# An encoder's ConvFFN on one core: partial sums seeded in PSUM, the down product in units between the up products

## The chip, the core and the metric

The kernel runs on one core of one Trainium2 chip. The metric is the device time of one execution in microseconds. TensorE's clock is granted at one of two levels, 1.2 or 2.4 GHz; the profile gives it as a share of the higher one.

## What is computed

Two layers of an encoder over 768 tokens of width 1024 (two requests of 512 and 256 tokens, six tiles of 128 tokens). Each layer has a mixer (latent attention beside a Fourier branch) and then the ConvFFN that the change touches:

```python
def conv_ffn(h, w_up, w_conv, b_conv, w_down):
    up = centred_dwconv(h @ w_up, w_conv, b_conv)
    a, b = jnp.split(up, 2, axis=-1)
    return (jax.nn.gelu(a, approximate=True) * b) @ w_down

h = rms_norm(x, g_ffn_pre[l]) * (1 + sc2) + sh2     # D_MODEL 1024, D_FF 2816
y = conv_ffn(h, w_up[l], w_conv[l], b_conv[l], w_down[l])
x = x + gt2 * rms_norm(y, g_ffn_post[l])
```

The scales, shifts and gates come from `silu(c) @ w_ada + b_ada`, six segments of 1024 columns per layer. All is float32; every product is made of three matmuls of split halves (high × high, high × low, low × high).

## The kernel before, in words

**Up products.** `ffn` works through 22 pairs `j` of 128 columns of `w_up`, one column block of the left half and one of the right. A pair is a two-by-two block product in seven products instead of eight: sums and differences of the four weight quarters (`up_weights`) times seven sums and differences of the input's quarters (`form_step`, kept in `S["FH"]`). A product (`prod` in `up_pair`) is 12 matmuls of up to 384 columns (L1311 to L1313) into one bank of PSUM. Products 0 and 2 share bank "a", 3 and 5 share "c", 1 is in "b", and 4 and 6 are in "d"; product 2 adds onto what 0 left in "a", product 5 onto what 3 left in "c", and product 6 onto "d". Between the two, the intermediate value is read out: `p1_` (ScalarE, L1334) copies the first sum to SBUF, `p6` (L1337), `p7` (L1343), `p5` (L1346), `p4` (L1349) and `p3` (L1354) are VectorE adds from PSUM and SBUF. Then come the convolution along the tokens (`conv`, L1224 to L1229) and `finish` (gelu, product, split), which leaves `G[j]`.

**Weights.** A pair's two raw blocks of `w_up` come by two transfers of 512 KB from the SyncE queue (L147). `l1x`, `s12`, `s3`, `s4` make four forms; three of them fill two blocks each (high part by ScalarE, L1258, low part by VectorE, L1259), the fourth fills one (L1281, L1282); the sums are on VectorE (L1267, L1268, L1273, L1278). Raw blocks, forms, down weights and several temporaries all come out of one pool of 20 blocks (`blk`, 128 x 1024 float32).

**Down product.** Every two pairs make a chunk (the last has four). `down_step` runs a chunk for one token tile into two fresh banks (L1389 to L1391), ScalarE copies the banks to a block (L1401) and GpSimd's queue adds the block onto `y_d` in DRAM (L1403 for the first chunk, L1405 after). A chunk's six steps stand behind the next pair's seven products. The last chunk reads `y_d` back (L501).

**Start and order.** The input's third column group (token tiles 4 and 5) is made late, by `h_last` (`form_step`: transposes L441, copies L444, sums and splits L453 to L463). So pairs 0 and 1 are split into a part of 256 and one of 128 columns, and `h_last` stands between pair 1's second and third product of 256 columns. Between the pairs stand "fillers", pieces of `ada_steps`, which form the scales and shifts on VectorE (L317, L319) from `w_ada` blocks.

`run` writes out the steps in this order, with the loads and splits of later weights in between: loads up to `RAWS` entries ahead, splits by a planned start (`LA_SPLIT`) and by how many blocks of the pool are free. Behind the first steps the framework orders the instructions of each engine by priority and readiness; on the chip each engine takes them in the order so fixed.

## Time and profile before

| | |
|---|---|
| three runs | 2407.21, 2408.55, 2416.14 us; median 2408.55 |
| profiled execution: its own time, its span | 2411.59 us, 2409.8 us |
| TensorE busy (matmul, weight load) | 96%, 86% of the span |
| VectorE, ScalarE, GpSimd busy | 67%, 45%, 10% |
| mean granted clock of TensorE | 0.971 |

Busy time is the share of the span in which the engine has an instruction under way. The matmuls of TensorE overlap in the rows, so what one costs is the distance from its start to the next one's. "Idle before" is the time in which the engine stood still ahead of an instruction, with the instruction whose end released it. All times are in us from the start of the span.

### The profile page before, as it was taken

The numbers are of one execution on the slowest core, as the hardware profiler recorded it, in microseconds if no ns is written. First come the engines' busy times: TensorE is split into PE (matmuls) and PEld (weight loads), VectorE is DVE, ScalarE is ACT, GpSimd is POOL, SyncE is SP. The second block draws the span as 40 slices with busy tenths as digits, with TensorE's granted clock in tenths as the row PEclk, the third lists the DMA queues.
The fourth block names the chain that finished last, engine by engine and source line by source line (L and its number), as shares of the span: only waits on it lengthen the run. The fifth ranks groups of instructions, "written<-read, shape, count | busy, mean of one in ns | idle before, by whom it ended". The sixth has DMA issues, their size and how long they took to land. (4 is left out here: it accounts for less than half of the span.)

```text
span 2409.8 us, 33324 instructions
## 1 busy us (share of the span) xinstructions
PE 2313.5 (96%) x12848; PEld 2072.9 (86%) x12848; DVE 1624.9 (67%) x2692; ACT 1076.8 (45%) x1844; POOL 249.1 (10%) x409
## 2 busy tenths in 40 slices
PE   8999999999999889989999999999999998999998
PEld 5888889988899788888878888899888998888897
DVE  5665557763767778777686755477637877766677
ACT  4423345541644444445454233355416445545452
POOL 1002000000111110111130020000001011011001
PEclk9999999999979999999999999999999799999999
DMA  9554431242236664656555544312423365556654
GB/s 260 151 170 134 133 104 32 71 156 94 88 97 180 158 166 114 149 135 146 142 184 151 171 134 133 104 32 68 158 95 97 93 181 147 116 113 145 151 123 175
DMA packets 262556, 316.24 MB, mean 131 GB/s; under 512 B 21436, under 2 KB 194150, under 8 KB 262397
## 3 DMA queue, kind: packets, MB, share of 16 engines
q1 hardware_dynamic: 240365, 235.85, 32.4%
q0 software_dynamic: 22032, 78.26, 14.8%
q8 instruction: 101, 1.65, 0.3%
q14 instruction: 58, 0.48, 0.1%
HBM read 225.89 MB, written 81.87 MB: 128 GB/s over the span
## 5 line engine op out<-in xcount | busy, mean ns | idle before, releaser
L1311 PE MATMUL ps<-d,w 128*128 128x384 f32 (+2 forms) x1344 | 463.0, 345 | 64.5 <-DVE r L1343 55.4
L1312 PE MATMUL ps<-d,w 128*128 128x384 f32 (+2 forms) x1344 | 458.7, 342 | 2.4 <-DVE d L454 2.4
L1313 PE MATMUL ps<-d,w 128*128 128x384 f32 (+2 forms) x1344 | 456.1, 341 | 0.0
L187 PE MATMUL ps<-d,w 128*128 128x512 f32 (+1 forms) x1152 | 393.4, 342 | 0.0
L188 PE MATMUL ps<-d,w 128*128 128x512 f32 (+1 forms) x1152 | 362.4, 337 | 0.0
L1311 PEld LDWEIGHTS ps<-d,w 128*128 128x128 f32 x1344 | 272.8, 203 | 77.7 <-DVE r L1343 60.8
L190 PE MATMUL ps<-d,w 128*128 128x512 f32 (+1 forms) x1152 | 296.4, 338 | 0.0
L159 DVE TENSOR_TENSOR w<-w,w 128x1024 fp32r<-128x1024 f32 (+3 forms) x164 | 192.3, 1178 | 141.6 <-ACT w L158 71.3
L1312 PEld LDWEIGHTS ps<-d,w 128*128 128x128 f32 x1344 | 273.2, 203 | 3.8 <-DVE d L454 2.8
L1313 PEld LDWEIGHTS ps<-d,w 128*128 128x128 f32 x1344 | 272.6, 203 | 0.0
L187 PEld LDWEIGHTS ps<-d,w 128*128 128x128 f32 x1152 | 216.2, 188 | 52.6 <-issue 3.4
L158 ACT ACTIVATE w<-w 128x1024 fp32r<-128x1024 f32 (+2 forms) x168 | 170.9, 1024 | 177.5 <-DVE w L159 47.2
L188 PEld LDWEIGHTS ps<-d,w 128*128 128x128 f32 x1152 | 216.6, 188 | 25.2
L1389 PE MATMUL ps<-w,d 128*128 128x512 f32 x528 | 206.1, 390 | 0.1
L1390 PE MATMUL ps<-w,d 128*128 128x512 f32 x528 | 206.0, 390 | 0.0
L1391 PE MATMUL ps<-w,d 128*128 128x512 f32 x528 | 205.7, 390 | 0.0
L319 DVE SCALAR_TENSOR_TENSOR w<-w,c,w 128x512 f32<-128x512 f32 x280 | 195.4, 745 | 11.7 <-DMA w<-in_w_ada_dram 11.7
L1259 DVE TENSOR_TENSOR w<-w,w 128x1024 fp32r<-128x1024 f32 x132 | 159.8, 1220 | 57.9 <-ACT w L1258 56.6
L1258 ACT ACTIVATE w<-w 128x1024 fp32r<-128x1024 f32 x132 | 137.2, 1054 | 126.2 <-DVE w L1268 70.7
L190 PEld LDWEIGHTS ps<-d,w 128*128 128x128 f32 x1152 | 178.3, 190 | 0.4
L1224 ACT ACTIVATE r<-r,v 128x768 f32<-128x768 f32 x88 | 90.6, 1030 | 175.5 <-DVE r L1349 127.3
L1401 ACT ACTIVATE w<-ps 128x512 f32<-128x512 f32 x216 | 126.6, 595 | 86.9 <-PE ps L1391 82.6
(253 smaller groups left out, 4118.7 us busy)
## 6 DMA issues: line engine op xcount, KB each, us to landing
y_d<-w POOLq DMA_DIRECT2D x108, 512.0 KB, 6.4
w<-in_w_up_dram SPq DMA_DIRECT2D x88, 512.0 KB, 5.5
w<-in_w_ada_dram SPq DMA_DIRECT2D x80, 512.0 KB, 4.3
w<-in_w_in_dram SPq DMA_DIRECT2D x48, 512.0 KB, 4.5
w<-in_w_down_dram SPq DMA_DIRECT2D x44, 512.0 KB, 5.7
xs<-w SPq DMA_DIRECT2D x18, 512.0 KB, 2.7
w<-xs SPq DMA_DIRECT2D x18, 512.0 KB, 4.6
w<-in_w_ada_dram SPq DMA_DIRECT2D x32, 256.0 KB, 5.6
```

Of the source, the lines that this page charges most:

```text
L158: nc.scalar.activation(out=o_(w.hi), in_=i_(w.raw), func=AF.Copy)
L159: (w.eng or nc.vector).tensor_sub(out=o_(w.lo), in0=i_(w.raw), in1=f(o_(w.hi)))
L187: nc.tensor.matmul(o, lh, rh[:, c0:c0 + s], start=(first and k == 0), stop=False)
L188: nc.tensor.matmul(o, lh, rl[:, c0:c0 + s], start=False, stop=False)
L190: nc.tensor.matmul(o, ll, rh[:, c0:c0 + s], start=False, stop=(last and k == n - 1))
L319: nc.vector.scalar_tensor_tensor(out=o, in0=x, scalar=c, in1=o, op0=ALU.mult, op1=ALU.add)
L1311: nc.tensor.matmul(ps, wh[:, k], x, start=(start and k == 0), stop=False, skip_group_check=True)
L1312: nc.tensor.matmul(ps, wh[:, k], y, start=False, stop=False, skip_group_check=True)
L1313: nc.tensor.matmul(ps, wl[:, k], x, start=False, stop=(k == 3), skip_group_check=True)
L1389: nc.tensor.matmul(ps, gh[:, cc], dw[j].hi[:, o], start=(j == all_js[0]), stop=False)
L1390: nc.tensor.matmul(ps, gh[:, cc], dw[j].lo[:, o], start=False, stop=False)
L1391: nc.tensor.matmul(ps, gl[:, cc], dw[j].hi[:, o], start=False, stop=(j == all_js[-1]))
```

## The change

- `up_weights` makes seven forms instead of four, each in one block (high part in the left half, low part in the right), each made and freed by itself.
- The order of the seven products of a pair is a, c, b, a, d, b, d. Their banks are held for the whole FFN. `p1_` copies bank a into bank b by ScalarE, and the next product adds onto it there; `p6` copies b into d in the same way; `p5` copies c to SBUF; `p7` and `p3` are VectorE adds with it, `p2` and `p4` plain ScalarE copies. `base` runs one matmul into b and one into d ahead of their first use in an FFN.
- Pair 1 is not split by columns any more, and `h_last` stands between the two parts of pair 0.
- The down product of each chunk but the last is cut into 12 units (a token tile and a half of the columns), which stand between the up products of the next two pairs, in three banks that are held. A unit of a later chunk begins with a ScalarE copy of its partial sum from SBUF into the bank and ends with a copy back; `Y`, six blocks, stays in SBUF, and `y_d` is gone. Its down weights come by halves, a block for two pairs.
- `ada_steps` takes `w_ada` in eight parts of 128 rows and 1024 columns instead of 256 rows and 512 columns.
- `form_step` makes its seven splits in the new order of the products.
- The pool has 21 blocks instead of 20, the pool of rows 6 instead of 7. `run` counts outstanding loads by blocks (`RAWS` 4, a pair counts 2, its later forms 0), and splits ahead of time only while four blocks (`SLACK`) are free.

```diff
-R_BUFS = 7
+R_BUFS = 6
-W_BUFS = 20
+W_BUFS = 21
+SLACK = 4
-RAWS = 3
+RAWS = 4
...
-    y_d = [[dp.tile([128, D], F32, name=f"y_d_{l}_{t}") for t in range(NT)] for l in range(L)]
...
-        ws = [[w_rows(a["w_ada"][l], 2 * i, 2, seg * D + half * 512, 512) for i in range(4)] for half in range(2)]
+        ws = [w_rows(a["w_ada"][l], k, 1, seg * D, D) for k in range(8)]
...
             def load():
                 for i, w in enumerate(A):
                     w_dma(w)
                     box[i] = w.raw
                     w.raw = None
-            us[0].load = load
+            us[0].load, us[0].raws = load, 2
             for u in us[1:]:
-                u.load = lambda: None
-
-            def two(u, z):
-                u.hi, u.lo = blk(F32R), blk(F32R)
-                nc.scalar.activation(out=u.hi, in_=z, func=AF.Copy)
-                nc.vector.tensor_sub(out=u.lo, in0=z, in1=f(u.hi))
...
+                u.load, u.raws = lambda: None, 0
+
+            def put(i, z):
+                w = us[i].home = blk(F32R)
+                us[i].hi, us[i].lo = w[:, 0:512], w[:, 512:1024]
+                nc.scalar.activation(out=us[i].hi, in_=z, func=AF.Copy)
+                nc.vector.tensor_sub(out=us[i].lo, in0=z, in1=f(us[i].hi))
+
+            def l11():
+                put(0, box[0][:, 0:512])
+
+            def s1():
+                z = box[2] = blk(F32)
+                nc.vector.tensor_add(out=z[:, 0:512], in0=box[1][:, 0:512], in1=box[1][:, 512:1024])
+                put(1, z[:, 0:512])
...
+                def base(name):
+                    if name not in PB:
+                        w = us[0].hi
+                        PB[name] = bank()
+                        nc.tensor.matmul(PB[name][:, 0:384], w[:, 0:128], w[:, 0:384], start=True, stop=True)
+                    return PB[name][:, 0:n]
+
                 def p1_(ps):
+                    nc.scalar.activation(out=base("b"), in_=ps, func=AF.Copy)
+
+                def p5(ps):
                     B["t"] = row(F32)
-                    B["u2"], B["u3"] = B["t"][:, 0:n], B["t"][:, 384:384 + n]
-                    nc.scalar.activation(out=B["u2"], in_=ps, func=AF.Copy)
+                    B["p5"] = B["t"][:, 0:n]
+                    nc.scalar.activation(out=B["p5"], in_=ps, func=AF.Copy)
 
                 def p6(ps):
-                    nc.vector.tensor_add(out=B["u2"], in0=ps, in1=B["u2"])
+                    nc.scalar.activation(out=base("d"), in_=ps, func=AF.Copy)
...
                 def p7(ps):
-                    nc.vector.tensor_add(out=B["u3"], in0=ps, in1=B["u2"])
...
+                    nc.vector.tensor_add(out=half(1, 1), in0=q3(ps), in1=q3(B["p5"]))
 
                 def p3(ps):
-                    nc.vector.tensor_add(out=half(0, 1), in0=q3(ps), in1=q3(B["u2"]))
+                    nc.vector.tensor_add(out=half(0, 1), in0=q3(ps), in1=q3(B["p5"]))
                     B.clear()
                     if end:
                         conv(j, 0, C.pop(0))
+
+                def p4(ps):
+                    nc.scalar.activation(out=half(1, 0), in_=q3(ps), func=AF.Copy)
+                    if end:
+                        conv(j, 1, C.pop(1))
                         finish(j)
...
-                return [prod("a", 0, 0, 0, True, p1_), prod("b", 1, 512, 1, True, p6), prod("a", 0, 512, 2, False, p2, (0,)),
-                        prod("c", 2, 0, 3, True, p7), prod("d", 1, 0, 4, True, p5, (1,)),
-                        prod("c", 2, 512, 5, False, p4, (2,)), prod("d", 3, 0, 6, False, p3, (3,))]
+                return [prod("a", 0, 0, True, p1_), prod("c", 1, 4, True, p5), prod("b", 2, 1, False, p6),
+                        prod("a", 3, 2, False, p2), prod("d", 4, 3, False, p7), prod("b", 5, 6, False, p3),
+                        prod("d", 6, 5, False, p4)]
...
+        def down_unit(c, i):
...
+            js = list(range(starts[c], starts[c + 1]))
+            t, half = i % 6, i // 6
+            dc = dwc[c][half]
+
+            def emit():
+                if c == 0:
+                    if i < 3:
+                        YB.append(bank())
+                    if t not in Y:
+                        Y[t] = blk(F32)
+                ps = YB[i % 3]
+                y = Y[t][:, half * 512:half * 512 + 512]
+                if c:
+                    nc.scalar.activation(out=ps, in_=y, func=AF.Copy)
...
+                nc.scalar.activation(out=y, in_=ps, func=AF.Copy)
...
-        early = [up_pair(j, uw[j], ((0, 2), (2, 3))) for j in range(2)]
-        out += early[0][0] + early[1][0][0:2] + [h_last] + early[1][0][2:] + early[0][1] + early[1][1]
...
+        early = up_pair(0, uw[0], ((0, 2), (2, 3)))
+        out += early[0] + [h_last] + early[1] + up_pair(1, uw[1])[0]
+        units = []
+        for j in range(2, NF):
+            st = up_pair(j, uw[j])[0]
+            if j % 2 == 0 and first[j - 2] < lc:
+                units = [down_unit(first[j - 2], i) for i in range(12)]
+            slots = [0, 0, 0, 1, 2, 1, 1] if j % 2 == 0 else [1] * 7
+            for i in range(7):
+                out.append(st[i])
+                for _ in range(slots[i] if units else 0):
+                    out.append(units.pop(0))
+                if i in (2, 6):
+                    out += fillers.pop(0) if fillers else []
...
-                due = k <= i + 1 or start[k] - now <= LA_SPLIT
+                due = k <= i or (k <= i + 1 or start[k] - now <= LA_SPLIT) and free_blocks() >= SLACK
...
-            while nd < len(order) and nd - ns < (RAWS if not s.hold else s.hold):
+            while nd < len(order) and (sum(w.raws for _, w in order[ns:nd]) + order[nd][1].raws
+                                       <= (RAWS if not s.hold else s.hold)):
```

## Rows read from the trace of the kernel before

**Rows 1.** The profile's page, its first line.

```profile
span 2409.8 us, 33324 instructions
```

**Rows 2.** Stage table: stretch, length, busy time (instructions) per engine, granted clock, DMA.

```profile
622.00:700.00 78.00, 73.27 (x429) 70.66 (x428) 64.56 (x105) 44.90 (x76) 11.20 (x14) 0.78 0.25 75
700.00:1190.00 490.00, 446.68 (x2266) 412.00 (x2266) 369.70 (x553) 229.78 (x315) 59.17 (x77) 0.95 0.60 150
...
1250.00:1830.00 580.00, 580.00 (x3399) 508.03 (x3398) 350.26 (x630) 230.93 (x467) 44.59 (x93) 1.00 0.38 114
1830.00:1905.00 75.00, 68.12 (x402) 65.46 (x401) 58.43 (x95) 41.69 (x72) 10.52 (x12) 0.77 0.33 98
1905.00:2375.00 470.00, 451.14 (x2347) 418.87 (x2346) 339.07 (x505) 236.32 (x323) 47.05 (x58) 0.99 0.58 143
```

**Rows 3.** TensorE's waits, 700 to 1190, then 1905 to 2375: total, times, longest.

```profile
PE ps L1311 <- DVE r L1343: 37.9, 7, 7.0
PE ps L1311 <- ACT r L1334: 3.3, 3, 1.8
...
PE ps L1311 <- DVE r L1343: 17.5, 9, 4.8
```

**Rows 4.** Timeline of TensorE, 780 to 793: start, duration, instruction, idle before.

```profile
786.78 0.69 PE L1311 MATMUL ps<-d,w 128*128 128x384 f32 x1 [5.26 <-DVE r L1343]
787.27 0.52 PE L1312 MATMUL ps<-d,w 128*128 128x384 f32 x1
787.59 0.52 PE L1313 MATMUL ps<-d,w 128*128 128x384 f32 x1
...
791.08 0.33 PE L1313 MATMUL ps<-d,w 128*128 128x384 f32 x1
...
792.99 0.33 PE L1312 MATMUL ps<-d,w 128*128 128x384 f32 x1
```

**Rows 5.** Timeline of VectorE, 780 to 787.

```profile
782.43 0.69 DVE L1267 TENSOR_TENSOR w<-w 128x512 f32<-128x512 f32 x1 [5.00 <-DMA w<-in_w_up_dram]
...
786.18 0.55 DVE L1343 TENSOR_TENSOR r<-ps,r 128x384 f32<-128x384 f32 x1
```

**Rows 6.** Waits of SyncE's load queue, 700 to 1190, then 1905 to 2375.

```profile
SPq L147 <- DMA y_d<-w: 114.1, 15, 19.7
...
SPq L147 <- DMA y_d<-w: 213.8, 15, 26.5
```

**Rows 7.** ScalarE's groups by line, 1905 to 2375: busy, mean ns, idle before.

```profile
L1401 ACT ACTIVATE w<-ps 128x512 f32<-128x512 f32 x108 | 64.1, 595 | 54.2 <-PE ps L1391 51.9
L1258 ACT ACTIVATE w<-w 128x1024 fp32r<-128x1024 f32 x56 | 57.8, 1053 | 28.2 <-DMA w<-in_w_up_dram 14.5 <-DVE w L1268 11.3 <-issue 1.5
...
L1281 ACT ACTIVATE w<-w 128x512 fp32r<-128x512 f32 x19 | 11.9, 628 | 16.9 <-DMA y_d<-w 15.8 <-DVE w L1259 1.1
...
L1334 ACT ACTIVATE r<-ps 128x384 f32<-128x384 f32 x19 | 9.0, 475 | 2.5 <-PE ps L1313 2.5
```

**Rows 8.** Timeline of TensorE at the start of layer 0's FFN, 640 to 702.

```profile
643.78 0.28 PE L1313 MATMUL ps<-d,w 128*128 128x256 f32 x1
...
646.66 0.28 PE L1313 MATMUL ps<-d,w 128*128 128x256 f32 x1
649.87 0.66 PE L441 MATMUL ps<-ident,w 128*128 128x128 f32 x4 [2.93 <-DVE w L493]
...
659.55 0.22 PE L1311 MATMUL ps<-d,w 128*128 128x128 f32 x1
...
670.06 0.41 PE L1311 MATMUL ps<-d,w 128*128 128x128 f32 x1
670.27 0.41 PE L1312 MATMUL ps<-d,w 128*128 128x128 f32 x1
...
693.10 0.63 PE L1311 MATMUL ps<-d,w 128*128 128x384 f32 x1
```

More of the change, by code (lines that the diff above doesn't have):

```diff
@@ L337, in finish @@
                                     in_=bg[64 * half:64 * half + 64:32, 0:512])
-        return [part(h, i) for h in range(2) for i in range(4)], Step(finish, 0.9)
+        return [part(k) for k in range(8)], Step(finish, 0.9)
     def ada_groups(*segs):
@@ L1244, in up_weights @@
             box = {}
-            us = [Weight([], 0) for _ in range(4)]
+            us = [Weight([], 0) for _ in range(7)]
             def load():
@@ L1272, in s3, with s2, l12 @@
+            def s2():
+                z = box[2]
+                nc.vector.tensor_sub(out=z[:, 512:1024], in0=z[:, 0:512], in1=box[0][:, 0:512])
+                put(2, z[:, 512:1024])
+            def l12():
+                put(3, box[0][:, 512:1024])
             def s3():
-                nc.vector.tensor_sub(out=box[1][:, 0:512], in0=box[0][:, 0:512], in1=box[1][:, 0:512])
-                two(us[2], box.pop(1))
+                z = box[1][:, 0:512]
+                nc.vector.tensor_sub(out=z, in0=box[0][:, 0:512], in1=z)
+                put(4, z)
@@ L1301, in part, with prod @@
                 B = {}
-                def prod(name, u, o, i, start, after=None, free=()):
+                def prod(name, u, i, start, after):
                     def emit():
-                        if start:
-                            B[name] = bank()
-                        ps = B[name][:, 0:n]
-                        (wh, wl), (xh, xl) = form(u, o), S["FH"][i]
+                        if name not in PB:
+                            PB[name] = bank()
+                        ps = PB[name][:, 0:n]
+                        wh, wl = (z.rearrange("p (k c) -> p k c", k=4) for z in (us[u].hi, us[u].lo))
+                        xh, xl = S["FH"][i]
                         for k in range(4):
@@ L1394, in emit @@
                     dw[j].hi = dw[j].lo = None
-                if c == lc:
-                    return
-                for t in ts:
-                    ps = S.pop(("yp", t))
-                    y = blk(F32)
-                    for half in range(2):
-                        nc.scalar.activation(out=y[:, half * 512:half * 512 + 512], in_=ps[half], func=AF.Copy)
-                    if c == 0:
-                        nc.gpsimd.dma_start(out=y_d[l][t], in_=y)
-                    else:
-                        nc.gpsimd.dma_start(out=y_d[l][t], in_=y, accum_op=ALU.add)
@@ L1406, in down_step @@
[L1406 removed]
+            return Step(emit, 6 * len(js) * len(ts) * 512 * MM_US, [dw[j] for j in js])
+        YB = []
+        dwc = [[Weight([((j - starts[c]) * 512, 512, a["w_down"][l][j * 128:(j + 1) * 128, h * 512:h * 512 + 512], None)
+                        for j in range(starts[c], starts[c + 1])], 1024) for h in range(2)] for c in range(lc)]
+        def down_unit(c, i):
[12 more added lines that the diff above has]
+                    nc.scalar.activation(out=ps, in_=y, func=AF.Copy)
+                cc = slice(t * 128, t * 128 + 128)
+                for j in js:
+                    o = slice((j - js[0]) * 512, (j - js[0]) * 512 + 512)
+                    gh, gl = G[j]
+                    nc.tensor.matmul(ps, gh[:, cc], dc.hi[:, o], start=(c == 0 and j == js[0]), stop=False,
+                                     skip_group_check=True)
+                    nc.tensor.matmul(ps, gh[:, cc], dc.lo[:, o], start=False, stop=False, skip_group_check=True)
+                    nc.tensor.matmul(ps, gl[:, cc], dc.hi[:, o], start=False, stop=(j == js[-1]),
+                                     skip_group_check=True)
+                nc.scalar.activation(out=y, in_=ps, func=AF.Copy)
+                if t == 5:
+                    dc.hi = dc.lo = None
+                if i == 11:
+                    for j in js:
+                        G.pop(j)
+                    if c == lc - 1:
+                        YB.clear()
+            return Step(emit, 3 * len(js) * 512 * MM_US, [dc])
```

94 lines of the change are left out of this document (30 added, 64 removed).

## The prediction, made before the changed kernel was run

> **What bounds the kernel now.** I read the stage table first [rows 2], then who makes TensorE wait in the two stretches where it waits [rows 3], then one such wait instruction by instruction on TensorE [rows 4] and on VectorE [rows 5], then what holds up the loads [rows 6], ScalarE [rows 7], and last the start of the FFN [rows 8].
>
> The stage table says that TensorE sets the time. Between the two FFNs (1250 to 1830) it is busy in all 580 us, at the full granted clock; nothing that the change does there can help, and it can only hurt if it takes work's cover away. The holes are in the FFNs: 490.00 − 446.68 = 43.3 us of layer 0's steady part and 470.00 − 451.14 = 18.9 us of layer 1's, and the two starts (622 to 700, 1830 to 1905) run at a mean clock of 0.78 and 0.77 [rows 2].
>
> Nearly all of the 62 us has one cause. TensorE, at an up product's first matmul (L1311), waits for the VectorE add L1343: 7 waits and 37.9 us in layer 0, 9 waits and 17.5 us in layer 1 [rows 3]. The reader should see why that add is so urgent. Products 3 and 5 of a pair share bank "c", so product 5 may not write until `p7` (L1343) has read what product 3 left; only product 4 lies between. A product is 12 matmuls 0.1735 us apart (eleven steps from 791.08 to 792.99) [rows 4], so the cover is 2.08 us. At 782.43 VectorE had just stood still for 5.00 us, with L1267 at its head, a sum over the second `w_up` block, whose load had not landed; L1267, three more sums and a split ran, and only then L1343, at 786.18 [rows 5]. TensorE resumed at 786.78, after 5.26 us idle, and on the lower clock: the matmuls start 0.32 us apart (787.27, 787.59) and are back at 0.17 by 791.08 [rows 4]. Some 11 of them at 0.32 instead of 0.1735 cost another 1.6 us. Why the load is late: the load queue stood for 114.1 us of layer 0's stretch and 213.8 us of layer 1's waiting for a `y_d` transfer, which held the block that the load was to go into [rows 6].
>
> **The change, part by part.**
>
> *Down partial sums.* 108 accumulating `y_d` transfers go, and with them the waits of [rows 6] as they stand; six blocks of the pool now hold `Y` for the whole FFN, against one block more in the pool. So the loads lose a slow partner and also some room. The last chunk no longer reads `y_d` back.
>
> *Wait of product 5.* In the new order, (a, c, b, a, d, b, d), each second use of a bank again has one product between, so the cover is the same 2.08 us. But the reader in between is now ScalarE three times (`p1_` copies a into b before product b; the same copy frees a; `p6` copies b into d before product d) and VectorE once (`p7` before the last d). The three adds `p6`, `p4` and old `p7` leave VectorE, at 0.55 us each [rows 5]. No weight sum stands in front of the ScalarE copies; weight copies that wait for loads do.
>
> What can be won here is what [rows 3 and 4] show: layer 0, 37.9 + 7 × 1.6 = 49.1 us; layer 1, 17.5 us and two waits long enough to drop the clock (1.6 each), 20.7 us. Sum 70 us.
>
> *The start.* Pair 1 is no longer split into a 256- and a 128-column part. In the trace the 128-column products run from 659.55 to 693.10, 33.6 us for 168 matmuls; on the low clock they go 0.21 us apart (670.06, 670.27) [rows 8]. One pair's 84 of them on the low clock are 17.9 us. Against that, pair 1's 84 matmuls of 384 columns take 84 × 0.1735 = 14.6 us, plus 1.6 us until the clock is back. But cover goes: pair 1's first two products (24 matmuls from 643.78 to 646.66, 2.88 us) ran ahead of `h_last` and its other five behind it, while ScalarE and VectorE made the third column group. Now TensorE reaches the transposes 2.9 us sooner, and they start when their rows are ready, at 649.87 as now; the idle time of 2.93 us becomes 5.8 us. Then nothing runs until `split(0)` has ended, by my estimate at about 658, a little before the 659.55 of now, since pair 1's splits no longer mix in. So: 658 + 17.9 + 16.2 = 692.1, against 693.1; if the clock stays high in the narrow part (84 × 0.12 at most, 10.1 us), 683 and less. Layer 1 is the same picture. Bounds per layer: a loss of 5 us (one more wait of the kind in [rows 4]) and a gain of 11 us. I take +3 each, near the low-clock end, because that is what this trace's narrow matmuls did: 6 us.
>
> *ScalarE's load.* In layer 1's stretch it is busy 236.32 of 470 us [rows 2]. Per pair come three more product copies at 0.475 us (L1334), six preloads of a PSUM bank, and seven half-size weight copies at 0.628 (L1281) for three of 1.053 (L1258) and one of 0.628. The preload, a copy from SBUF into PSUM, is in no row; its cost lies between nothing and the 0.628 of L1281, and I take L1401's 0.595, which has the same 512 columns through PSUM the other way [rows 7]. Together 1.43 + 3.57 + 0.61 = 5.6 us per pair, 112 us in 20 pairs: ScalarE goes from 50% to about 77% of a stretch of 450 us. It stays below TensorE, but is no longer idle half of the time when a product ends.
>
> ScalarE's own waits for loads matter now as VectorE's did. In layer 1 they come to 14.5 us (L1258) and 15.8 us (L1281) [rows 7], 30.3 us, and I put layer 0 at the same, 60 us in both. A copy of 0.475 us behind such a wait has 2.08 − 0.475 = 1.6 us of cover. If loads stay as late as now and about half of the waiting is under that cover, 30 us are left; if they come early enough, nothing. Loads start further ahead (four blocks outstanding, counted as blocks) and have no `y_d` beside them, but the pool is tighter: half, 15 us.
>
> The Trainium skill (TensorE: Matmul & The Clock Gate, section "Architectural detail: the array is 16× 32×32, not 1× 128×128") says that ScalarE and VectorE take instructions strictly first in, first out; the trace agrees for VectorE, where an add with its data long there stood behind a sum without. By that rule a copy behind a waiting weight copy can't overtake it, and the 15 us would be nearer to the 30.
>
> *What stays on VectorE.* `p7` and `p3`, and `finish(j)`: the down units of a chunk now start after four products of the next pair (8.3 us after the pair that they need has ended), where before they started after all seven. VectorE is busy 369.70 of 490 us in layer 0 [rows 2], and in a stretch that is 40 us shorter with 1.65 us less per pair it is at about 75%. Bounds: none, or as much per wait as layer 1 shows now, 17.5 / 9 = 1.9 us, in each of 20 chunks, 39 us. I take half, 20 us.
>
> *The rest at nothing:* the two dummy matmuls per FFN of `base` (0.3 us each, among the idle time at the start); ada parts in half as many instructions over the same columns, VectorE work in stretches where TensorE is fully busy; `R_BUFS` 6, the `SLACK` rule and `RAWS` in the mixer and attention, hidden under TensorE's 580 busy us. Should that cover go, one wait as in [rows 4] costs 7 us.
>
> *Sum:* 70 + 6 − 15 − 20 = 41 us. The profiled execution took 2411.6 us for a span of 2409.8 [rows 1], so 2370.6 for its like; the median shown is 3 us lower: **2367 us**.
>
> **The rivals.**
>
> *ScalarE becomes the queue that TensorE waits for (slower).* Place: `p1_` and `p6`, each between two products with 2.08 us of cover. For it: 77% load, first in first out, and preload, evacuation, weight copies and the identity pass of the convolution (1 us pieces) all in that queue. Against it: TensorE's present waits for ScalarE are short, 3 of them and 3.3 us in layer 0 [rows 3]. If each of the two copies ends late by one weight copy and itself (1.053 + 0.475 = 1.53 us) in all 44 pairs, that is 134 us against the 76 of gain: 2408 + 58 = 2466 us. It decides from 76 / 44 = 1.7 us of new waiting per pair.
>
> *The load stays late.* In layer 0 the ada loads share the pool with `Y`; with six blocks gone for good the next `w_up` load again waits for a block and VectorE's sum again for the load. For it: the queue waits in [rows 6] are for blocks, not for bandwidth. Against it: a block held by a transfer is what goes away. Then layer 0's 49 us stay, and 21 + 6 − 20 is left: 2401 us.
>
> *The waits go altogether.* 70 + 6 and nothing new: 2332 us. For it: ScalarE has slack; against it: each pair has four turns of one bank between engines.
>
> **How the numbers follow.** The forecast 0.60, ScalarE 0.15, the load 0.13, all gone 0.12. The range goes from just under the full gain to just above no change, 2330 to 2412: it leaves out most of the ScalarE case and a twentieth below. The forecast's own range is 2340 to 2392, from the two halves that I took going to either bound. A measurement of this kernel can tell about 0.5% (12 us) from no change: faster 0.74 (the forecast, all gone, and a third of the load case), same 0.11, slower 0.15.
>
> **What would show it.** Right: no TensorE wait over 3 us in the two steady stretches, and no clock below 0.97 there; idle TensorE under 25 us in the two; the 128-column matmuls half as many, with a longer hole ahead of them; no `y_d` transfers; ScalarE at 70 to 80% in the steady part. Wrong: waits of an up product for a ScalarE copy of more than 1 us in most pairs (ScalarE rival), or L1267's successor standing for a `w_up` load with the load queue waiting for matmuls or splits to free a block (load rival). The prediction also fails if the mixer's stretch is longer than its 580 us, which would be the pool sizes and the new rule for splits.

## The result, and the profile after

The changed kernel takes 2314.0 us (median of 4 runs, 2312.1 to 2316.4) against 2410.0 us: ratio 0.9599, 95% interval 0.9578 to 0.962. That is 96 us faster, more than twice the 41 us forecast and below the low end of the range.

The profile's page begins with the span, 97.2 us shorter than in [rows 1]:

```profile
span 2312.6 us, 32983 instructions
```

The stage table of the changed kernel, cut at its own stages, answers to [rows 2]:

```profile
622.00:700.00 78.00, 71.26 (x386) 67.32 (x385) 60.73 (x98) 48.83 (x96) 10.16 (x14) 0.85 0.26 82
700.00:1130.00 430.00, 430.00 (x2263) 397.46 (x2262) 343.80 (x509) 314.16 (x525) 12.05 (x23) 1.00 0.34 100
1190.00:1770.00 580.00, 580.00 (x3399) 507.94 (x3399) 340.68 (x568) 232.93 (x474) 44.72 (x80) 1.00 0.39 118
1771.00:1840.00 69.00, 61.29 (x334) 59.60 (x333) 60.00 (x94) 41.91 (x81) 6.54 (x8) 0.80 0.25 81
1840.00:2280.00 440.00, 440.00 (x2313) 409.42 (x2312) 311.46 (x476) 316.87 (x531) 3.89 (x7) 1.00 0.27 81
```

Both steady stretches are full: 430 of 430 us and 440 of 440 us of TensorE at the full clock. ScalarE is busy 73% and 72% of them, VectorE 80% and 71%. What is left of TensorE's waits answers to [rows 3]; these are the four longest sums from 622 us to the end (three more, 4.0 us together, are ahead of transposes, L393), and all of them lie in the starts and the tails:

```profile
PE ps L439 <- DVE w L491: 5.0, 3, 4.3
PE ps L1315 <- ACT d L451: 3.4, 2, 3.2
PE ps L1315 <- ACT ps L1341: 3.3, 3, 1.6
PE ps L1315 <- DVE r L1355: 2.5, 1, 2.5
```

The start of layer 0's FFN on TensorE's timeline, for [rows 8]:

```profile
646.47 1.12 PE L439 MATMUL ps<-ident,w 128*128 128x128 f32 x4 [4.27 <-DVE w L491]
...
653.25 0.33 PE L1315 MATMUL ps<-d,w 128*128 128x128 f32 x1
...
670.29 0.41 PE L1317 MATMUL ps<-d,w 128*128 128x128 f32 x1
670.51 0.63 PE L1315 MATMUL ps<-d,w 128*128 128x384 f32 x1
...
673.17 0.49 PE L1317 MATMUL ps<-d,w 128*128 128x384 f32 x1
673.49 0.35 PE L1315 MATMUL ps<-d,w 128*128 128x384 f32 x1
...
694.84 0.39 PE L1430 MATMUL ps<-w,d 128*128 128x512 f32 x1
```

The 84 narrow matmuls that are left take 17.3 us (653.25 to 670.51), where the 168 took 33.6. The first down matmul stands behind four products (8.3 us) of pair 2, so that pair began at 686.5.

ScalarE's groups in 1840 to 2280, for [rows 7]; L1425 is the seed written into PSUM, L1341 the copy of one bank into another:

```profile
L1258 ACT ACTIVATE w<-w 128x512 fp32r<-128x512 f32 x131 | 81.1, 625 | 14.4 <-PE ps L1317 7.7 <-DVE w L1266 3.1 <-DVE w L160 1.5
L1435 ACT ACTIVATE w<-ps 128x512 f32<-128x512 f32 x107 | 63.1, 590 | 40.4 <-PE ps L1433 40.2
L1425 ACT ACTIVATE ps<-w 128x512 f32<-128x512 f32 x96 | 57.4, 598 | 1.9
...
L1341 ACT ACTIVATE ps<-ps 128x384 f32<-128x384 f32 x19 | 9.2, 483 | 1.3 <-PE ps L1317 1.3
```

No idle time of ScalarE in the two steady parts ends with a transfer any more.

**Where the 97 us came from.** From the first up matmul to the start of pair 2 (here the first down matmul less 8.3 us): 6.3 us in layer 0, 5.9 in layer 1. From there to the end of each FFN: 61.8 and 26.0 us. The mixer and attention between the FFNs became 3.1 us longer (598.3 to 601.4, from layer 1's first mixer matmul to its first up matmul). Before the first FFN 0.3 us. The sum is 97.2. For the largest part, one window from pair 2 to the end of each FFN, of the kernel before and then of the changed one:

```profile
693.10:1238.37 545.27, 500.23 (x2518) 458.94 (x2518) 410.08 (x619) 257.28 (x372) 78.78 (x100) 0.95 0.59 151
1900.24:2409.80 509.56, 482.89 (x2481) 445.17 (x2481) 370.29 (x564) 247.91 (x351) 53.52 (x71) 0.98 0.56 141
```

```profile
686.50:1170.00 483.50, 482.14 (x2518) 442.82 (x2517) 382.09 (x568) 340.59 (x581) 29.22 (x46) 1.00 0.34 104
1829.08:2312.60 483.52, 475.73 (x2482) 440.29 (x2480) 347.19 (x540) 331.62 (x565) 10.56 (x20) 1.00 0.26 82
```

TensorE's idle time fell from 45.0 to 1.4 us and from 26.7 to 7.8 us; the same number of matmuls took 18.1 us less in layer 0 and 7.2 us less in layer 1. The trace's record of the granted clock accounts for this: in these two windows of the kernel before, TensorE worked 37.5 and 12.6 us at 1.2 GHz, behind many of its waits and at the start of pair 2, half of which is lost against 2.4 GHz; in the changed kernel it did no work at that level there. So 62.6 us are waiting and 25.3 us are slow matmuls.

### The profile page after: what moved, and what is told of

The parts are those of the page before. It is cut to its first block, busy times and chain, and to the rows that moved or that the text cites. A ratio compares the mean times of both kernels' runs of the same rounds, so it can differ in the third digit from the quotient of the medians.

```text
span 2312.6 us, 32983 instructions
## 1 busy us (share of the span) xinstructions
PE 2273.0 (98%) x12684; PEld 2035.8 (88%) x12684; DVE 1557.9 (67%) x2516; ACT 1250.2 (54%) x2302; POOL 165.8 (7%) x301
## 5 line engine op out<-in xcount | busy, mean ns | idle before, releaser
L1315 PE MATMUL ps<-d,w 128*128 128x384 f32 (+2 forms) x1288 | 435.1, 338 | 9.3 <-ACT d L451 3.4
L1316 PE MATMUL ps<-d,w 128*128 128x384 f32 (+2 forms) x1288 | 434.5, 337 | 0.1
L1317 PE MATMUL ps<-d,w 128*128 128x384 f32 (+2 forms) x1288 | 433.3, 336 | 0.0
L1315 PEld LDWEIGHTS ps<-d,w 128*128 128x128 f32 x1288 | 251.1, 195 | 23.0 <-ACT d L451 4.2
L188 PEld LDWEIGHTS ps<-d,w 128*128 128x128 f32 x1152 | 216.2, 188 | 52.6 <-issue 3.4
L1316 PEld LDWEIGHTS ps<-d,w 128*128 128x128 f32 x1288 | 251.0, 195 | 9.6 <-DVE d L452 0.3
L159 ACT ACTIVATE w<-w 128x1024 fp32r<-128x1024 f32 (+2 forms) x168 | 171.5, 1024 | 159.9 <-DVE w L317 31.6
L1259 DVE TENSOR_TENSOR w<-w,w 128x512 fp32r<-128x512 f32 x308 | 206.4, 686 | 69.1 <-ACT w L1258 67.0
L1317 PEld LDWEIGHTS ps<-d,w 128*128 128x128 f32 x1288 | 251.0, 195 | 0.9 <-DVE w L1259 0.8
L189 PEld LDWEIGHTS ps<-d,w 128*128 128x128 f32 x1152 | 216.6, 188 | 25.7 <-DVE d L195 0.6
L1258 ACT ACTIVATE w<-w 128x512 fp32r<-128x512 f32 x308 | 189.1, 626 | 45.2 <-PE ps L1317 17.0
L317 DVE SCALAR_TENSOR_TENSOR w<-w,c,w 128x1024 f32<-128x1024 f32 x140 | 174.1, 1276 | 15.1 <-DMA w<-in_w_ada_dram 15.0
L191 PEld LDWEIGHTS ps<-d,w 128*128 128x128 f32 x1152 | 178.2, 190 | 0.2
L1435 ACT ACTIVATE w<-ps 128x512 f32<-128x512 f32 x216 | 127.5, 590 | 86.9 <-PE ps L1433 86.0
L1433 PE MATMUL ps<-w,d 128*128 128x512 f32 x432 | 171.3, 397 | 0.0
L1432 PE MATMUL ps<-w,d 128*128 128x512 f32 x432 | 170.5, 395 | 0.0
L1430 PE MATMUL ps<-w,d 128*128 128x512 f32 x432 | 167.6, 389 | 0.0
L1225 DVE SCALAR_TENSOR_TENSOR r<-r,v,r 128x511 f32<-128x511 f32 (+1 forms) x176 | 100.6, 613 | 34.1 <-ACT r L1222 33.9
```

The lines of the kernel that those rows point to most:

```text
L188: nc.tensor.matmul(o, lh, rh[:, c0:c0 + s], start=(first and k == 0), stop=False)
L189: nc.tensor.matmul(o, lh, rl[:, c0:c0 + s], start=False, stop=False)
L191: nc.tensor.matmul(o, ll, rh[:, c0:c0 + s], start=False, stop=(last and k == n - 1))
L1258: nc.scalar.activation(out=us[i].hi, in_=z, func=AF.Copy)
L1259: nc.vector.tensor_sub(out=us[i].lo, in0=z, in1=f(us[i].hi))
L1315: nc.tensor.matmul(ps, wh[:, k], x, start=(start and k == 0), stop=False, skip_group_check=True)
```

## The experiments

The theory after the result: the sum that no longer goes through DRAM frees blocks, so loads come in time and the two queues that feed TensorE no longer stand. Rivals: the finer weight blocks, the order and seeds of the products, the counting of loads, the rule of four free blocks (`SLACK`), the pools, the modulation's loads, the units spread between products.

### One part of the change undone

**Loads counted by entries.**

```diff
-RAWS = 4
+RAWS = 3
...
-            us[0].load, us[0].raws = load, 2
+            us[0].load = load
```

> The changed kernel, with one part undone: outstanding loads are counted by entries again, three at a time, a pair's later forms included. Load theory (the long waits went because the w_up blocks now land before their first reader): ScalarE and VectorE stand again for w_up loads, TensorE idles 20 us or more in the two steady parts, 2335 to 2400 us. Turn theory (they went because ScalarE instead of a VectorE add stands between two uses of a bank): a late load still has to block ScalarE's queue, but the copies are mostly ahead of it; 2314 to 2325 us. Cover theory (the down units between the products give the readers more time): like the turn theory, under 2325 us.

Measured 2311.0 us, ratio 0.9581 (0.9554 to 0.9609). The counting is worth nothing here.

**Units in one piece behind the pair.**

```diff
-            slots = [0, 0, 0, 1, 2, 1, 1] if j % 2 == 0 else [1] * 7
+            slots = [0] * 6 + [12 if j % 2 == 0 else 0]
```

> The changed kernel with all 12 down units of a chunk in one row behind the next pair, as before, instead of between the products. Cover theory: the seven products of a pair stand back to back again with 2.08 us between two uses of a bank, and preload and evacuation of the units follow each other on ScalarE in the row (1.2 us per unit of 1.36 us); waits of 1 to 3 us come back in most pairs, 2340 to 2400 us. Load theory and turn theory: within 10 us of the changed kernel, 2314 to 2325 us.

Measured 2317.5 us, ratio 0.9609 (0.9581 to 0.9636). The 3 us more lie within the two intervals; no long wait returned.

**Old order of the products, with VectorE's additions in fresh banks.**

```diff
-                return [prod("a", 0, 0, True, p1_), prod("c", 1, 4, True, p5), prod("b", 2, 1, False, p6),
...
+                return [prod("a", 0, 0, True, p1_), prod("b", 2, 1, True, p6, (1,)), prod("a", 3, 2, False, p2),
```

> The changed kernel with the old order of the seven products, the old VectorE adds and fresh banks a, b, c, d for each pair; forms in one block each, down units, loads counted by blocks and start stay. Turn theory: the wait for the add between products 3 and 5 comes back, VectorE has 1.65 us more per pair; 2340 to 2400 us. Load theory and cover theory: the adds find their turn in time, 2314 to 2330 us.

Measured 2314.4 us, ratio 0.9596 (0.9568 to 0.9623), with VectorE busy 86% of 700 to 1130 us and TensorE all of it. Not the cause by itself.

**Weight forms in pairs of blocks.**

```diff
-            us = [Weight([], 0) for _ in range(7)]
+            us = [Weight([], 0) for _ in range(4)]
...
-            for u, fn in zip(us, (l11, s1, s2, l12, s3, s4, l22)):
+            for u, fn in zip(us, (l1x, s12, s3, s4)):
```

> The changed kernel with one part undone: the weight forms of an up pair again in four steps, three of them with a block for the high and a block for the low halves of two forms, freed only when the later form is used. If the finer blocks are what keeps the loads and splits of the next pair on time, PE's waits in the steady parts come back and the run lands near 2380 us or above. If the sum that no longer goes through DRAM is enough by itself, PE stays busy through 700 to 1130 us and the time stays within 0.5% of 2314 us.

Measured 2320.6 us, ratio 0.961 (0.9595 to 0.9624): nothing that stands clear of the changed kernel's interval.

**The sum through the DRAM scratch again.**

```diff
-                    nc.scalar.activation(out=ps, in_=y, func=AF.Copy)
...
+                        nc.gpsimd.dma_start(out=y_d[l][t], in_=y, accum_op=ALU.add)
...
+                            Y[t] = load_x(y_d[l][t])
...
+                pend = [down_step(first[j], [t]) for t in range(NT)]
```

> The changed kernel with one part undone: the sums of the down products again go out by GpSimd's accumulating transfers to the DRAM scratch, a whole chunk behind the next pair, from blocks of the pool, and are read back for the last chunk; forms, seeds of the up products, start and counting of loads are those of the changed kernel. If those transfers are the cause (blocks held until they have landed, and the queues shared with the loads), the waits of PE in the steady parts come back and the run takes 2375 to 2400 us. If the block per form is the cause, it stays within 0.5% of 2314 us.

Measured 2319.6 us (2311.2 to 2324.1), ratio 0.9597 (0.9572 to 0.9623). The edit also puts the chunk back in one piece and its down weights back in rows. This fells my theory in its simple form. Its stage row, 700 to 1130, and then the time that its load queue stood for the sum's transfers, there and in 1900 to 2270:

```profile
700.00:1130.00 430.00, 425.59 (x2232) 393.13 (x2231) 335.90 (x499) 258.03 (x424) 54.83 (x73) 1.00 0.67 167
```

```profile
SPq L149 <- DMA y_d<-w: 117.8, 14, 29.4
SPq L149 <- DMA y_d<-w: 36.9, 10, 7.9
```

In layer 0 the load queue stands for the sum's transfers as long as in [rows 6]; in layer 1 it stands 36.9 us, where the kernel before has 184.1 in the same stretch. The 108 transfers land in 6.4 us (median) as they did, and a `w_up` load needs 5.9 us where it needed 5.5 in the kernel before (4.3 in the changed one). Yet TensorE is idle only 4.4 us in layer 0. That a queue working ahead stands for a block doesn't say that anyone needs the block soon.

**The start cut as before.**

```diff
-        early = up_pair(0, uw[0], ((0, 2), (2, 3)))
-        out += early[0] + [h_last] + early[1] + up_pair(1, uw[1])[0]
+        early = [up_pair(j, uw[j], ((0, 2), (2, 3))) for j in range(2)]
+        out += early[0][0] + early[1][0][0:2] + [h_last] + early[1][0][2:] + early[0][1] + early[1][1]
```

> The changed kernel with the start of each FFN undone: pair 1 is again cut into 256 and 128 columns around the last step of the forms. If the start is worth what the two traces say (6.3 and 5.9 us), it takes 2326 us, ratio to the kernel before about 0.965. If those 12 us come from the loads and not from the cut, it stays at 2314 us.

Measured 2331.6 us, ratio 0.9656 (0.9642 to 0.9671): 17.6 us above the changed kernel by the medians, which come from two rounds, some 14 us by the ratios, with the steady parts full. In the traces its two starts are 10.5 and 6.0 us longer than the changed kernel's. The start is a part of the gain of its own.

**No rule of four free blocks.**

```diff
-                due = k <= i or (k <= i + 1 or start[k] - now <= LA_SPLIT) and free_blocks() >= SLACK
+                due = k <= i + 1 or start[k] - now <= LA_SPLIT
```

> The changed kernel with one part undone: a split that is due within a step or 10 us is again put into the queues of ScalarE and VectorE whether or not four blocks are free. If the rule is what keeps those two queues from standing behind a block that is not free yet, PE's waits in the steady parts come back: 2360 to 2400 us. If it is not needed, since the blocks are free anyway, 2314 us within 0.5%.

Measured 2314.8 us, ratio 0.9601 (0.9586 to 0.9616). Not needed by itself.

### One part alone put into the kernel before

**Loads counted by blocks** (the reverse of the first edit).

> The kernel before, with one part done alone: outstanding loads counted by blocks, four at a time, a pair counts two and its later forms nothing. Load theory: most of the 7 waits of 5 to 7 us in layer 0 go; 2340 to 2370 us, against 2410. If it is the y_d transfers that hold the blocks, counting can't help, as the load queue waits for the block anyway: 2390 to 2415 us. Turn theory and cover theory: no gain, 2400 us or more.

Measured 2411.5 us, ratio 0.9989 (0.9977 to 1.0001): nothing in time. But what the engines stand for has changed. The largest waits for transfers of ScalarE and VectorE in 700 to 1130, in the kernel before and then in this run (L1259 and L1260 are its split):

```profile
ACT w L1258 <- DMA w<-in_w_up_dram: 24.4, 8, 7.6
DVE w L1267 <- DMA w<-in_w_up_dram: 17.1, 5, 5.5
```

```profile
ACT w L1259 <- DMA y_d<-w: 35.6, 8, 8.0
DVE w L1260 <- DMA y_d<-w: 18.5, 5, 5.5
```

The loads are there in time, and now the splits stand for a block that the sum's transfers hold.

**The sum kept on the chip.** Forms, products, loads, start and pools stay.

```diff
-                        nc.gpsimd.dma_start(out=y_d[l][t], in_=y, accum_op=ALU.add)
...
+                if c:
+                    nc.scalar.activation(out=ps, in_=y, func=AF.Copy)
...
+                pend = [down_unit(c, i) for i in range(12)]
```

> The kernel before with one part of the change alone: the sum of the down products stays in six blocks on the chip and is put into three held PSUM banks by ScalarE, the twelve units of a chunk in one piece behind the next pair; forms, products, loads, start and pools are those of the kernel before. If the transfers of the sum are the whole cause, the waits are gone and only the start (12 us) is missing: 2322 to 2340 us. If a block per form is needed as well, since six blocks fewer are left for weights, it stays near or above the kernel before, 2390 to 2430 us.

Measured 2362.9 us, ratio 0.9786 (0.9772 to 0.9801). Its steady parts are nearly full:

```profile
700.00:1130.00 430.00, 423.88 (x2201) 384.87 (x2200) 353.52 (x534) 269.30 (x400) 11.52 (x22) 1.00 0.32 96
1900.00:2270.00 370.00, 369.43 (x1924) 338.51 (x1923) 274.29 (x403) 247.11 (x366) 1.15 (x2) 1.00 0.25 75
```

That is between the two outcomes. Alone it takes away most of the waiting, though in the changed kernel it could be missed. Both can be true only if other parts of the change do the same work. The run also pays at its end: 23.0 us pass after its last matmul, where the kernel before and the changed kernel have 7.7 and 7.8. The two blocks of the last gate are loaded from 2336.51, when VectorE's add (L1457) releases them; the changed kernel issues these loads at 2272.43 and 2284.41, 40 and 28 us before its end.

```profile
2336.51 1.18 POOL L371 DMA_DIRECT2D w<-mod_d  x2 [0.86 <-DVE w L1457]
```

Without these 15 us the part alone would, as an estimate, be worth some 67 us instead of 52.

**The rule of four free blocks.**

> The kernel before with one part of the change alone: splits wait in the plan until four blocks are free, unless the step itself needs them. If the rule is the cause by itself, only the start (12 to 17 us) is missing: 2326 to 2345 us. If the blocks are short because the sum's transfers hold them, the rule has nothing to give and may put the splits later still: 2400 to 2440 us.

Measured 2414.7 us, ratio 1.0011 (0.9997 to 1.0025): nothing.

**A block per weight form** (with the counting by blocks).

> The kernel before with a block per weight form (and the loads counted by blocks, which alone was worth nothing: ratio 0.9989); order and additions of the products, the sum's transfers, start and pools as before. If the blocks that come free earlier are enough by themselves, 2330 to 2360 us. If the sum's transfers are what holds the loads, 2395 to 2412 us.

Measured 2377.0 us, ratio 0.9858 (0.9842 to 0.9874), between the two outcomes. In layer 1 the waits are all but gone (367.70 of 370 us busy from 1900), in layer 0 they are not (402.05 of 430 from 700). One of those left, on ScalarE's timeline and then on TensorE's:

```profile
941.55 1.15 ACT L1261 ACTIVATE w<-w 128x512 fp32r<-128x512 f32 x2 [3.90 <-DMA y_d<-w]
942.61 0.47 ACT L1339 ACTIVATE r<-ps 128x384 f32<-128x384 f32 x1
```

```profile
943.13 0.69 PE L1318 MATMUL ps<-d,w 128*128 128x384 f32 x1 [6.16 <-ACT r L1339]
```

Two weight splits (L1261) stand at the head of ScalarE for 3.90 us until a transfer of the sum gives back the block that the first of them writes into. Behind them stands the copy `p1_` (L1339), and TensorE waits 6.16 us for that copy. It is [rows 4 and 5] again, with the block in place of the load and ScalarE in place of VectorE.

**The sizes of the pools.**

```diff
-R_BUFS = 7
+R_BUFS = 6
...
-W_BUFS = 20
+W_BUFS = 21
```

> The kernel before with the sizes of the two pools alone: 21 blocks and 6 rows in place of 20 and 7. If the kernel before stood so close to the edge of its blocks that one more is enough, 2360 to 2385 us, and the waits of its queue of loads on the transfers of the sum shrink. If the pools are not it, 2405 to 2417 us, and the modulation's loads, or several of the small parts together, are left.

Measured 2434.2 us, ratio 1.0102 (1.0085 to 1.0118): 24 us slower, neither of the two outcomes expected. All of it is in layer 1, whose FFN is 28.8 us longer (layer 0's is 4.0 shorter):

```profile
700.00:1130.00 430.00, 394.70 (x2015) 363.25 (x2014) 329.49 (x498) 198.00 (x276) 50.35 (x68) 0.96 0.61 150
1900.00:2270.00 370.00, 339.33 (x1735) 315.66 (x1734) 255.34 (x376) 175.26 (x244) 35.61 (x44) 0.96 0.56 130
```

In that stretch the split of the down weights (L158) stands for the sum's transfers, which it never did there in the kernel before (11.5 us, all for its own load). Its waits for them, and the longest with what it costs TensorE:

```profile
ACT w L158 <- DMA y_d<-w: 18.9, 4, 5.6
2142.05 1.06 ACT L158 ACTIVATE w<-w 128x1024 fp32r<-128x1024 f32 x1 [5.57 <-DMA y_d<-w]
2144.89 0.69 PE L1311 MATMUL ps<-d,w 128*128 128x384 f32 x1 [7.19 <-DVE r L1343]
```

### Several parts undone together in the changed kernel

**Scratch, and no rule of four free blocks.**

> The changed kernel with two parts undone together: the sum goes through the DRAM scratch as before, and the splits are issued without the rule of four free blocks. Each part of the change tried so far could be undone alone at no cost. If either of these two is enough to take the waits away, undoing both brings back some 50 to 70 us: 2360 to 2395 us. If neither is the cause, it stays at 2311 to 2325 us, as with the scratch alone.

Measured 2318.1 us, ratio 0.9612 (0.9597 to 0.9627): not this pair.

**Scratch, and old products.**

> The changed kernel with two parts undone together: the sum through the DRAM scratch, and the old order of the products with VectorE's additions in fresh banks. If it is the queues of ScalarE and VectorE, standing behind a split whose block a transfer still holds, that delay the additions which PE waits for, then the old turn (p7 on VectorE behind p1 on ScalarE) is the other half of the cause: 2345 to 2365 us. If the order of the products is worth nothing here either, 2315 to 2325 us.

Measured 2331.6 us, ratio 0.9671 (0.9657 to 0.9685): between the two outcomes. The old products cost nothing with the sum on the chip and some 12 us beside the transfers (18 by the ratios).

**Scratch, and forms in pairs of blocks.**

> The changed kernel with two parts undone together: the sum through the DRAM scratch, and the weight forms in pairs of blocks. If blocks in short supply are the cause, and either six of them no longer sent out or forms freed one by one were enough, undoing both brings the waits back: 2345 to 2390 us. If the blocks are not what is short, 2315 to 2330 us.

Measured 2343.7 us, ratio 0.9718 (0.9703 to 0.9733), just under the first outcome. Undone alone these two cost nothing clear of the interval (ratios 0.9597 and 0.961, against 0.9599); together they cost some 29 us.

**Scratch, old products and pairs of blocks.**

> The changed kernel with all three undone, so that only the start, the pools, the loads of the modulation, the counting and the rule of four free blocks stay: if the three are the whole cause beside the start, 2410 less 12 to 17: 2390 to 2400 us. If pools or modulation loads carry a part, 2330 to 2380 us.

Measured 2341.8 us, ratio 0.971 (0.9694 to 0.9727). The three are not the whole cause beside the start: 70 us of gain are left. On top of the other two the old products cost nothing.

**The modulation's loads undone as well** (on top of those three).

```diff
-        ws = [w_rows(a["w_ada"][l], k, 1, seg * D, D) for k in range(8)]
+        ws = [[w_rows(a["w_ada"][l], 2 * i, 2, seg * D + half * 512, 512) for i in range(4)] for half in range(2)]
```

> The run with scratch, old products and two-block forms (2341.8 us) with one more part undone: the modulation's weights loaded again as two row blocks of 512 columns, added in four pieces of VectorE. If these loads and additions carry the steady part of layer 0, its FFN goes from 559 to 590 to 600 us and the run to 2370 to 2385 us, with layer 1 as it was (552 us). If the pools, the counting and the rule together carry it, the run stays at 2335 to 2350 us.

Measured 2355.3 us, ratio 0.9765 (0.9741 to 0.9789): 13.5 us more, between the two outcomes, with layer 0's row at 409.51 of 430 us busy where the run before it had 417.57. What is left of the change in this run is the start, the pools, the rule and the counting, and it is 56 us faster than before: 14 to 18 for the start, if it is worth the same here, and some 40 for pools, rule and counting together, which alone gave +24, +2 and −2 us.

### ScalarE's margin

Every seed written twice:

```diff
-                if c:
+                for _ in range(2 if c else 0):
                     nc.scalar.activation(out=ps, in_=y, func=AF.Copy)
```

> The changed kernel with every seed of a down unit written twice by ScalarE: 96 more writes of 0.60 us in each layer, 57 us in some 490 us, so that ScalarE is busy 85% where it was 73%. The theory that it stands well clear of the path says 2314 us within 1% and waits of PE on the seeds of 1 us at most; the rival, ScalarE as the queue that sets the pace, says that each added write costs its 0.6 us: 2314 + 115 = about 2430 us.

Measured 2315.6 us, ratio 0.9599 (0.9585 to 0.9613). The row of layer 0, and the seeds in it:

```profile
700.00:1130.00 430.00, 430.00 (x2261) 397.13 (x2260) 344.57 (x509) 360.32 (x621) 11.50 (x22) 1.00 0.33 99
```

```profile
L1425 ACT ACTIVATE ps<-w 128x512 f32<-128x512 f32 x192 | 114.5, 599 | 3.5
```

ScalarE is busy 84% of the stretch and TensorE still never waits. The rival in which ScalarE sets the pace is far off.

### The runs side by side

For each run ("before, X" is the kernel before with X put in alone, "after, X" the changed kernel with X undone), in 700 to 1130 us (layer 0) and 1900 to 2270 us (layer 1): "stood" is the time that ScalarE and VectorE together stood idle until a transfer ended, added up from their lists of waits; "idle" is the stretch less TensorE's busy time. All in us. The medians are of different rounds, in which the kernel before took 2409.8 to 2414.9 us.

| run | median | stood, idle: layer 0 | layer 1 |
|---|---|---|---|
| before | 2410.0 | 57.2, 37.7 | 49.9, 14.4 |
| before, pools | 2434.2 | 62.6, 35.3 | 54.6, 30.7 |
| before, rule | 2414.7 | 57.1, 39.3 | 54.3, 14.4 |
| before, counting | 2411.5 | 80.9, 34.1 | 25.6, 15.8 |
| before, block per form | 2377.0 | 43.2, 27.9 | 9.3, 2.3 |
| before, sum on chip | 2362.9 | 22.5, 6.1 | 8.0, 0.6 |
| after, scratch + products + pairs + modulation | 2355.3 | 38.4, 20.5 | 10.7, 6.6 |
| after, scratch + pairs | 2343.7 | 26.8, 11.6 | 20.9, 11.7 |
| after, scratch + products + pairs | 2341.8 | 15.7, 12.4 | 20.5, 7.9 |
| after, scratch + products | 2331.6 | 35.5, 16.6 | 4.2, 2.0 |
| after, start | 2331.6 | 2.1, 0 | 0, 0 |
| after, scratch | 2319.6 | 17.6, 4.4 | 1.3, 1.3 |
| after, scratch + rule | 2318.1 | 14.9, 5.3 | 1.5, 0.9 |
| after, pairs of blocks | 2320.6 | 7.2, 0.9 | 0, 0 |
| after, units in one piece | 2317.5 | 1.1, 1.8 | 0, 0.9 |
| after (every seed written twice) | 2315.6 | 1.6, 0 | 0, 0 |
| after, rule | 2314.8 | 5.4, 0 | 0, 0 |
| after, old products | 2314.4 | 2.7, 0 | 0, 0 |
| after, counting | 2311.0 | 16.5, 0 | 2.8, 0 |
| after | 2314.0 | 1.9, 0 | 0, 0 |

Read the two numbers of a stretch together. The runs that stand long idle long, whatever part of the change they have; where ScalarE and VectorE stand under 10 us in a stretch, TensorE is idle 2.3 us at most. This is one currency for all the parts. It is not exact (80.9 us of standing with 34.1 idle, 15.7 with 12.4, 16.5 with none), since what is queued behind the standing instruction differs.

That the waits come from this standing can be followed in the trace of the kernel before: from each TensorE wait over 0.5 us in 700 to 1190 and 1905 to 2375 back to the engine that released it, and along that engine's queue to where it last stood. Of 61.3 us, 59.5 end at a transfer: 47.1 at a `w_up` load, 10.7 at a load of down weights, 1.7 at a transfer of the sum. In the run with the counting alone, in the stretches of the table, 46.3 of 49.2 us end at a transfer of the sum.

## Why the prediction was wrong

**The sum 70 + 6 − 15 − 20 = 41.** Its last two terms failed. I charged 15 us for ScalarE and 20 us for VectorE, half of what I took as upper bounds: the first on the ground that loads might stay about half as late as before, the second because `p7`, `p3` and `finish` stay on VectorE and the down units follow sooner. Measured: no idle time of ScalarE ended with a transfer in the steady parts, 1.9 us of VectorE's did in layer 0 and 0.6 in layer 1, and TensorE waited for neither engine there: 0 and 0. With these at nothing the sum is the rival "the waits go altogether", 2332 us, to which I gave 0.12. The range that I gave as the forecast's own, 2340 to 2392, doesn't follow from the two halves going to either bound, which is 2332 to 2401; nor do the chances of "faster" add up to 0.74, but to 0.76.

The Trainium skill's rule of strict order in ScalarE and VectorE (TensorE: Matmul & The Clock Gate, "Architectural detail: the array is 16× 32×32, not 1× 128×128") spoke for the charge. The trace agrees with the rule: in the run with a block per form, `p1_` stood behind a split that itself stood for 3.90 us. But the rule says what a wait does once it is there, not that there is one.

**The 70 us were mis-sized**: 87.8 measured (61.8 + 26.0). The idle time was 62.6 us, where the waits that I had listed for it were 55.4; I left out the short waits that [rows 3] show in part. The slow clock was 25.3 us, where I had 11.2 + 3.2. By the trace's record of the clock, it fell eight times in layer 0's steady stretch and three times in layer 1's, where I counted seven and two, and cost 16.0 and 4.7 us there, 2.0 and 1.6 each; the rest lies outside these stretches. Per microsecond of idle time, 0.4 us came on top. The ScalarE waits of 30.3 us from which I charged were also short: [rows 7] leave out the split of the down weights, which stood another 14.2 us for its load in that stretch, and five of TensorE's nine waits over 0.5 us in layer 1's stretch go back to it.

**The start was mis-sized**: 6 us forecast, 12.2 between the two traces, 14 to 18 when it is undone alone. Most of the narrow products ran on the low clock as I said, 0.21 us apart, and the hole ahead of the transposes was 4.3 us where I had 5.8. The step that failed is the 658 us at which I let them begin: they began at 653.25. Of these 4.75 us, 3.4 were won ahead of the transposes, which I let start at 649.87 as before and which started at 646.47. That pair 1's copies and sums no longer stand among the splits of the last column group is my explanation, argued and not tried alone.

**ScalarE's load was right**: 77% forecast, 73 and 72% measured. I took 0.595 us for the seed that no row showed; it takes 0.598, and there were 96 in the stretch where I had 120. The run with doubled seeds shows that the ScalarE rival deserved less than 0.15.

**The mixer** at nothing cost 3.1 us, by the two traces. I did not follow it further: the changed kernel's runs with the scratch have it at 596.5 us, those without at 599 to 601, and the sum on the chip alone brings the kernel before from 598.3 to 602.2. So it goes with the sum on the chip; how is not shown.

**The reason given** for the late load, a block held by the sum's transfer [rows 6], was half right. It is shown that the sum kept on the chip takes most of the waiting away by itself (52 us in the kernel before, in spite of its longer end). It is also shown that it isn't needed: with the transfers back, all 108 of them, the load queue stands for them in layer 0 as long as before and 2320 us remain. And coming early is not enough for a load, as the counting alone shows: then the splits stand for blocks instead. The forms in single blocks (35 us alone, with the counting), the order of the products, the modulation's loads and the pools with the rule and counting each give back some of the same room, and in the changed kernel the sum on the chip, the forms or the order can each be missed alone. So the gain does not divide into parts; only the start stands by itself. What the runs share is how long ScalarE and VectorE stand in front of a transfer, be it a load that is late or a transfer that holds a block.

**Open:** why the sizes of the pools alone make the split of the down weights stand for the sum's transfers and cost 24 us, and which of pools, rule and counting hold the 40 us that they have together. One row fewer and one block more were not tried apart, nor the rule with the pools alone. Whether the modulation's loads gain by their shape or by VectorE's shorter work (per load, two additions of 1.276 us in place of four of 0.746) was not tried either. No version beat the changed kernel clearly: the counting by entries, at 0.9581, lies within its interval.

## What to carry to other kernels

A queue that works ahead shows long waits whether or not they hurt; look instead at how long the in-order engines that feed the bound engine stand idle in front of a transfer, and what is queued behind them. When a change relieves one shortage in several ways, undoing one part at a time shows nothing of any of them: put parts alone into the old kernel as well, and undo them in groups. And price a wait of TensorE with the slow matmuls behind it, from the busy time of a whole stretch, and charge a new wait only where something in the changed queue has a reason to be late.

## What the runs showed of the hardware

ScalarE writes 512 columns into PSUM in 0.598 us and reads them out in 0.590 us (L1425 and L1435 above); a copy of 384 columns from bank to bank takes 0.483 us, about as long as one into SBUF (0.475 in [rows 7]). So a running sum can go back into PSUM at the price of one copy each way.

The clock fell, and stayed low, while TensorE worked, not only when it stood still. In the changed kernel's start, TensorE is busy nearly throughout the narrow products. The granted clock is at 2.4 GHz for the first of them (0.11 us apart), falls to 1.2 GHz at 656.4 in the midst of them, and is back at 2.4 GHz at 673.5, in the 384-column products that follow (673.49 in the timeline above):

```profile
654.00:670.00 16.00, 15.65 (x81) 15.19 (x81) 15.23 (x27) 10.62 (x22) 0.00 (x0) 0.58 0.33 99
674.00:690.00 16.00, 16.00 (x95) 16.00 (x94) 13.04 (x21) 9.51 (x15) 2.90 (x6) 1.00 0.35 101
```
